# Holding the conditioning products of a hybrid decoder step behind two later norms

## The chip, the core and the metric

The kernel runs on one core of one Trainium2 chip. The metric is the device time of one execution in microseconds (us); smaller is better. The kernel before took 1204.66 us (median of three runs, 1202.11 to 1207.32). The engines are called PE (TensorE, the matrix products), DVE (VectorE), ACT (ScalarE), POOL (GpSimd) and SP (SyncE, which issues the DMA loads here).

## The reference

One step of a two-layer decoder for a prompt of 256 tokens and eight samples of four tokens each, 288 tokens in all, with a model width of 1024. Layer 0 mixes tokens by a gated delta rule (GDN), layer 1 by a state-space model (SSM). Each mixer is followed by a gated feed-forward part (FFN). Every part has a norm ahead of it, and each norm and each result is scaled and shifted by vectors made from a condition `c`:

```python
cs = jax.nn.silu(c)
for i in range(DEPTH):
    mod = cs @ p['w_mod'][i] + p['b_mod'][i]
    sh1, sc1, gt1, sh2, sc2, gt2 = [m[:, None, :] for m in jnp.split(mod, 6, axis=-1)]
    h = _rmsnorm(x, p['norm_mix'][i]) * (1 + sc1) + sh1
    ...
    x = x + gt1 * out
    h = _rmsnorm(x, p['norm_ffn'][i]) * (1 + sc2) + sh2
    x = x + gt2 * _swiglu(h, p['ffn_w_gate_up'][i], p['ffn_w_down'][i])
y = _rmsnorm(x, p['norm_final'])
```

Here `cs @ w_mod` gives twelve vectors (two layers, six each), the conditioning products. They hang on `c` alone and not on `x`, so that each may be computed at any time before its vector is used.

## The kernel before, in words

The activations stay on the chip, transposed: `x` has the 1024 channels as eight blocks (`k`) of 128 partitions by 288 tokens. The norm's output stands twice, `hh` and `hl`, a number rounded to the fast matmul format and what the rounding left over. Weights stream from memory.

**Weight chunks.** `chunk_load` (L267) takes 512 KB: four blocks of 128 rows by 256 columns. SP issues the load (L271) into a raw tile (`rw`, six tiles, shared with the conditioning loads). ACT writes the rounded copy `wh` (L87, four tiles), DVE the rest `wl` = `rw` - `wh` (L75, two tiles). `dense_chunk` (L285) then makes three products for each block and half: `wh` by `hh`, `wl` by `hh`, `wh` by `hl`; 24 in a chunk, into the accumulator `pd`. A chunk can be loaded and converted ahead with `load_early` (L282); `load32` (L361) does so for a 32-column piece.

**Stages.** In order: the first norm and the GDN mixer (to about 405 us, its output projection behind it), FFN0 (to 662), the SSM mixer (to 959), FFN1, and the final norm. The norms at the four seams are called norm 1 to norm 4 here: norm 3 stands between FFN0 and SSM, norm 4 between SSM and FFN1.

**A norm.** `Norm.add(k)` (L201) is called for every block of `x` as its projection ends: ACT squares the block, DVE adds it to `acc`. With the last block PE adds over the partitions by two products with ones into `ss` (the second is `self.mm`). Then `rstd` (L217) on ACT: logarithm, a load of the table of functions, exponential. `apply` (L223) goes on for each block: DVE makes `hu` (the scaled block), ACT `hh`, DVE `hl`. `hs` is the same for the sample tokens. The next stage's first product waits for the first `hh`. `apply` may issue an early chunk ahead of a given block (argument `at`).

**Conditioning products.** `mod_steps` (L147) is a generator for one vector: eight loads `wm` of 512 KB (L153), then after each second load a burst of eight calls on PE (`burst`, L64, at high priority), and as the last thing a tail: a copy `mt` on ACT, two transposes `pt` on PE, an addition on DVE. A vector has eight steps. `fill(n)` (L185) goes on by n steps, `ensure(r)` goes on to the end of the r-th vector. The vectors are made in the order in which they are used.

**What sets the order.** The code is written as generators which `weave` (L307) mixes in given shares; the SSM mixer's mix is a table of text lines, in which "m8" stands for eight steps of the conditioning products. The program order so made is given to a list scheduler, which sets each engine's final order by priority, with two means to bend it: `high_priority` and `issue_after`, which holds what is issued under it behind a given instruction. Tiles come from pools with a fixed number of buffers; a load waits until the tile's last reader is done.

Around norm 3, before, the calls were `ensure(8)`, `load32`, and an early chunk in `apply` at block 0. Around norm 4, before, there was one early chunk in `apply`, at block 4. The first steps of the next vectors came with `fill(4)` at the beginning of `ssm` and `fill(6)` at the beginning of FFN1.

Of the kernel before, what the change touches and what calls it, by code (L numbers as in the profile page):

```python
# [7 lines left out]
F32 = mybir.dt.float32  # L8
# [6 lines left out]
P = 128  # L15
NP_ = 256
# [4 lines left out]
KD = DM // P  # L21
# [6 lines left out]
def tile_hybrid_step(ctx: ExitStack, tc: tile.TileContext, I, O):  # L28
# [112 lines left out]
    def raw_tile(name):  # L141
        return wp.tile([P, 1024], F32, tag="raw", name=name, bufs=6)

    def sqt(name):
        return wp.tile([P, NT], F32, tag="sq", name=name, bufs=3)

    def mod_steps(l, s, m):  # L147

        pmod = pss.tile([P, 256], F32, tag="s", name=f"mod{l}{s}")
        rs_ = []  # L150
        for k in range(KD):
            r = raw_tile(f"wm{l}{s}{k}")
            SY.dma_start(r, I["w_mod"][l, k * P:(k + 1) * P, s * DM:(s + 1) * DM])  # L153
            rs_.append(r)
            if k % 2:

                burst([lambda q=q, k=k, r=r_: mm(pmod[32 * q:32 * q + 32, :], csT[:, k, :], r[:, 256 * q:256 * q + 256],
                                                 start=(k == 1), stop=(k == KD - 2))
                       for k, r_ in ((k, rs_[1]), (k - 1, rs_[0])) for q in range(4)])
                rs_.clear()  # L160
            if k < KD - 1:
                yield
        mt = sqt("mt")[:, 0:256]
        cp(mt, pmod)
        pt = pm([P, 2, P], "pt")
        for h in range(2):
            T.transpose(pt[:, h, :], mt[:, h * P:(h + 1) * P], ident)
        tt(m.rearrange("p (q h) r -> p h q r", h=2),
           pt.rearrange("p h (q r) -> p h q r", q=4)[:, :, :, 0:9],
           bmodT[:, l, s, :].rearrange("p (q h) -> p h q", h=2).unsqueeze(3).to_broadcast([P, 2, 4, 9]), ADD)  # L170
        if s in (1, 4):
            nw = nmix(l) if s == 1 else nffn(l)
            stt(m, m, 1.0, nw.unsqueeze(2).to_broadcast([P, KD, 9]), ADD, MUL)
        yield
# [10 lines left out]
    def fill(n=1):  # L185
        while n > 0 and todo:
            try:
                next(todo[0])
                n -= 1
                done[0] += 1  # L190
            except StopIteration:
                todo.pop(0)

    def ensure(rounds):
        fill(8 * rounds - done[0])
# [84 lines left out]
    early = {}  # L280

    def load_early(W, c0, k0, nk):  # L282
        early[c0, k0] = chunk_load(W, c0, k0, nk, 0)
# [23 lines left out]
    def weave(*work):  # L307

        work = [(w[0], w[1], w[2] if len(w) > 2 else 0) for w in work if w[0] is not None]
        top = max(n for _, n, _ in work)  # L310
        done = [0] * len(work)
        for i in range(1, top + 1):
            for w, (g, n, off) in enumerate(work):
                while done[w] * top < i * n:
                    done[w] += 1
                    if off:
                        with tc.high_priority(offset=off):
                            next(g, None)
                    else:
                        next(g, None)  # L320
        for g, _, off in work:
            for _ in g:
                pass
# [19 lines left out]
    def mods(n):  # L343
        for _ in range(n):
            fill(1)
            yield
# [181 lines left out]
    def gdn(gt1, nrm):  # L528
# [524 lines left out]
        ensure(6)  # L1053
        gst.close()

    def ffn(l, gt2, prev, nrm, late, n_late, n_mods):
        fst = ExitStack()
        fp = fst.enter_context(tc.tile_pool(name=f"ffn{l}", bufs=1))
        ah = fp.tile([P, KF, NT], F32R, name="ah")
        al = fp.tile([P, KF, NT], F32R, name="al")  # L1060
        W, WD = I["ffn_w_gate_up"][l], I["ffn_w_down"][l]
        def main():
            for p_ in range(KF // 2):
                pg, pu, gs = [], [], []
                yield from dense_g(pg, W, p_ * 256, KD, hh, hl)
                for m in range(2):
                    t = fp.tile([P, NT], F32, tag="gs", name="gs", bufs=4)
                    act(t, pg[m], AF.Silu)
                    gs.append(t)
                yield from dense_g(pu, W, FFN + p_ * 256, KD, hh, hl)  # L1070
                for m in range(2):
                    k = 2 * p_ + m
                    t = gs[m]
                    tt(t, t, pu[m], MUL)
                    cp(ah[:, k, :], t)
                    tt(al[:, k, :], t, ah[:, k, :].bitcast(F32), SUB)
            yield from out_proj(WD, ((0, KF),), KF, ah, al, gt2, nrm)

        work = late(fst)
        with prev.behind():  # L1080
            next(work)
        fill(n_mods[0])
        n_mods[1] = n_mods[1] if l == 0 else 96 - done[0]
        weave((main(), 136), (work, n_late), (mods(n_mods[1]), n_mods[1] + n_mods[2]) if n_mods[1] > 0 else (None, 0))
        fst.close()

    def late_tile(lp, name):
        return lp.tile([P, 1024], F32R, tag="st", name=name, bufs=4)

    def pattern(lp, src, outs, coefs, n, nm, vw=None):  # L1090
# [5 lines left out]
        for i, (o, (c_, m_)) in enumerate(zip(outs, coefs)):  # L1096
            u = (late_tile(lp, nm + "u")[:, 0:n] if i else t[:, n:2 * n]).bitcast(F32)
            act(u, src, AF.Copy, scale=m_)
            stt(o, vw(h_.bitcast(F32)), c_, vw(u), MUL, ADD)

    def late_gdn(fst):
        lp = fst.enter_context(tc.tile_pool(name="lateg", bufs=1))
        selB = lp.tile([P, 4, P], F32, name="selB")
        G.memset(selB, 0.0)
        for q in range(4):
# [42 lines left out]
    def ssm(gt1, nrm):  # L1148
# [320 lines left out]

        s0 = s0_products()  # L1470
        seq = chain_gens
        fill(4)
        weave((decays(), 6), (seq(*[bc_pair(p_) for p_ in range(4)]), 29), (mods(4), 18))
        smp_ = sample()
        proj = out_proj(I["ssm_w_out"][0], ((0, 12), (12, 16)), 16, yh, yl, gt1, nrm)
# [2 lines left out]
                     p=(lambda n: take(proj, n), 0),  # L1478
                     Z=(lambda n: mix(z_pair(n // 100, n // 10 % 10), 5, take(smp_, n % 10), n % 10), 9))
        for g, (line, more, side, smore, nc_, np_, tag) in enumerate((  # L1480
# [5 lines left out]
            main, n = plan(line, kinds)  # L1486
            side, m = plan(side, kinds)
            weave((core(g - 1, tag) if g else None, nc_), (main, n + more),
                  (prep(g) if g < 4 else None, np_), (side if m else None, m + smore))
        for _ in proj:  # L1490
            pass
        ensure(11)
        gst.close()

    def late_ssm(fst):
# [56 lines left out]
    nrm = Norm()  # L1552
# [92 lines left out]
    ffn(0, gt2, prev, nrm, late_gdn, 36, [6, 10, 9])  # L1645

    sh1, sc1, gt1, sh2, sc2, gt2 = mods1
    ensure(8)
    early[5120, 32] = load32(I["ssm_w_in"][0], 5120)
    nrm.apply(sc1, sh1, None, I["ssm_w_in"][0], 4096, (0,))  # L1650
    nrm = Norm()
    ssm(gt1, nrm)
    nrm.apply(sc2, sh2, None, I["ffn_w_gate_up"][1], 0, (4,))
    fin = ctx.enter_context(tc.tile_pool(name="fin", bufs=1))

    class Final:
# [35 lines left out]

    prev, nrm = nrm, Final()
    final[0] = nrm
    ffn(1, gt2, prev, nrm, late_ssm, 36, [6, 0, 9])
    nrm.finish()


# [28 lines left out]
```

## Time and profile before

| | |
|---|---|
| median of three runs | 1204.66 us (1202.11 to 1207.32) |
| the profiled execution | 1205.62 us |
| its span, first to last instruction | 1204.0 us |
| mean granted clock of PE | 0.979 of full |
| PE busy | 1138.1 us (95%) |
| DVE busy | 853.3 us (71%) |
| ACT busy | 629.8 us (52%) |

Times in the profile count from the start of the span. In a timeline a row gives the start, the time to the end, engine, line, operation, what is written from what, how many such instructions follow one another, and in brackets how long the engine had stood idle and what it had waited for. A row with a count shows a whole group. A burst of conditioning calls appears as 16 instructions, since each of the eight calls issues two.

### The profile page before, as it was taken

What the parts mean: (1) busy time and instruction counts of PE and PEld (TensorE: products, weight loads), DVE (VectorE), ACT (ScalarE), POOL (GpSimd) and SP (SyncE); (2) the same over time, 40 slices, a digit from 0 to 9 for tenths busy, and PEclk for the clock granted to TensorE, in tenths of its full rate; (3) what the DMA queues carried; (4) which work ended last, traced back from release to release, by engine and by line L of the source; (5) the groups of instructions that cost most, each with busy time, mean ns of one, the idle gap of its engine ahead of it and who ended that gap; (6) DMA issues with size and microseconds to landing.
All of it is one profiled execution on the core that took longest, in us unless ns stands there. A gap on an engine that the chain in (4) does not pass through costs nothing.

```text
span 1204.0 us, 23141 instructions
## 1 busy us (share of the span) xinstructions
PE 1138.1 (95%) x8634; PEld 1028.2 (85%) x8634; DVE 853.3 (71%) x2064; ACT 629.8 (52%) x1331; POOL 101.1 (8%) x273
## 2 busy tenths in 40 slices
PE   5899999999999999999999899999989989999996
PEld 3689778888978889999999788778869989999996
DVE  2878797888767785666664786678886787666654
ACT  3587445556544473434343675778734484444432
POOL 3121112122100100000000111001100010000000
PEclk8999999999999999999999899999989999999999
DMA  8765696633354689888655768667564579887771
GB/s 305 258 197 174 184 273 201 203 119 104 104 172 150 209 267 285 253 263 246 223 185 174 230 187 252 172 198 236 163 205 144 175 232 308 250 261 235 211 214 54
DMA packets 266724, 249.05 MB, mean 207 GB/s; under 512 B 12180, under 2 KB 252257, under 8 KB 266612
## 3 DMA queue, kind: packets, MB, share of 16 engines
q1 hardware_dynamic: 265980, 247.50, 66.4%
q8 instruction: 68, 1.11, 0.4%
q14 instruction: 44, 0.36, 0.1%
q10 hardware_dynamic: 632, 0.07, 0.0%
HBM read 226.64 MB, written 20.90 MB: 206 GB/s over the span
## 4 chain that ended last, share of the span: by engine, by line
PE 74%; DMA 9%; DVE 8%; ACT 6%; issue 2%; POOL 0%; SPq 0%; ACTq 0%; DVEq 0%; POOLq 0%
PE pd L62 56%; PE pch L62 4%; PE mod L62 3%; DMA wm<-in_w_mod_dram 3%; DMA D<-scumd 2%; DVE wl L75 1%; DVE cva L72 1%; ACT D L82 1%; DMA rw<-in_gdn_w_in_dram 1%; PE lu L62 1%; DMA rw<-in_ssm_w_in_dram 1%; ACT wh L87 1%; PE py L62 1%; DMA PP<-cumd 1%; DMA rw<-in_ffn_w_gate_up_dram 1%
## 5 line engine op out<-in xcount | busy, mean ns | idle before, releaser
L62 PE MATMUL pd<-hh,wh 128*128 128x288 f32 x1424 | 433.8, 306 | 10.6 <-ACT hh L87 9.1
L62 PE MATMUL pd<-hh,wl 128*128 128x288 f32 x1424 | 428.5, 301 | 2.5 <-DVE wl L75 2.5
L62 PE MATMUL pd<-hl,wh 128*128 128x288 f32 x1424 | 426.1, 301 | 1.7 <-DVE hl L72 1.5
L75 DVE TENSOR_TENSOR wl<-rw,wh 128x1024 fp32r<-128x1024 f32 (+2 forms) x258 | 309.9, 1201 | 163.6 <-PE pd L62 120.7
L87 ACT ACTIVATE wh<-rw 128x1024 fp32r<-128x1024 f32 (+2 forms) x258 | 267.9, 1040 | 270.2 <-PE pd L62 159.6
L62 PEld LDWEIGHTS pd<-hh,wh 128*128 128x128 f32 x1424 | 270.6, 190 | 27.9 <-issue 15.6
L62 PEld LDWEIGHTS pd<-hh,wl 128*128 128x128 f32 x1424 | 270.8, 190 | 6.0 <-DVE wl L75 3.8
L62 PEld LDWEIGHTS pd<-hl,wh 128*128 128x128 f32 x1424 | 270.6, 191 | 4.6 <-DVE hl L72 1.9
L62 PE MATMUL pd<-ah,wh 128*128 128x288 f32 x352 | 105.4, 299 | 0.0
L62 PE MATMUL pd<-al,wh 128*128 128x288 f32 x352 | 104.4, 297 | 0.0
L62 PE MATMUL pd<-ah,wl 128*128 128x288 f32 x352 | 104.4, 297 | 0.0
L72 DVE SCALAR_TENSOR_TENSOR cva<-ext,vT,cva 128x312 f32<-128x312 f32 x168 | 85.0, 537 | 8.9 <-ACT cva L82 8.3
L62 PEld LDWEIGHTS pd<-ah,wh 128*128 128x128 f32 x352 | 66.2, 188 | 1.2
L62 PEld LDWEIGHTS pd<-ah,wl 128*128 128x128 f32 x352 | 66.2, 188 | 0.0
L62 PEld LDWEIGHTS pd<-al,wh 128*128 128x128 f32 x352 | 66.2, 188 | 0.0
L62 PE MATMUL mod<-wm,csT 128*32 128x256 f32 x768 | 55.8, 415 | 8.1 <-DMA wm<-in_w_mod_dram 7.5
L62 PEld LDWEIGHTS mod<-wm,csT 128*32 128x32 f32 x768 | 21.5, 115 | 28.9 <-DMA wm<-in_w_mod_dram 11.0
L462 POOL COPY cvo<-ext 128x27 f32<-128x27 f32 x56 | 25.0, 446 | 220.0 <-ACT ext L87 219.4
L72 DVE SCALAR_TENSOR_TENSOR s0u<-s0u,elS,lu 128x128 f32<-128x128 f32 x128 | 36.3, 342 | 8.9 <-PE lu L62 8.5
L72 DVE SCALAR_TENSOR_TENSOR h0u<-h0u,elP,lsu 128x128 f32<-128x128 f32 x128 | 36.2, 342 | 7.4 <-PE lsu L62 6.5
L62 PE MATMUL pd<-ogh,wl 128*128 128x288 f32 x128 | 39.2, 307 | 2.2 <-DVE wl L75 2.2
L62 PE MATMUL pd<-ogh,wh 128*128 128x288 f32 x128 | 39.7, 311 | 0.0
(534 smaller groups left out, 1781.8 us busy)
## 6 DMA issues: line engine op xcount, KB each, us to landing
wm<-in_w_mod_dram SPq DMA_DIRECT2D x96, 512.0 KB
rw<-in_ffn_w_gate_up_dram SPq DMA_DIRECT2D x88, 512.0 KB
rw<-in_gdn_w_in_dram SPq DMA_DIRECT2D x48, 512.0 KB
rw<-in_ffn_w_down_dram SPq DMA_DIRECT2D x40, 512.0 KB
rw<-in_ssm_w_in_dram SPq DMA_DIRECT2D x40, 512.0 KB
s<-in_state_gdn_dram SPq DMA_DIRECT2D x16, 512.0 KB
rw<-in_gdn_w_out_dram SPq DMA_DIRECT2D x16, 512.0 KB
s0u<-in_state_gdn_dram SPq DMA_DIRECT2D x16, 512.0 KB
```

The lines of the kernel that those rows point to most:

```text
L62: return T.matmul(out, lhsT=lhsT, rhs=rhs, start=start, stop=stop)
L72: return V.scalar_tensor_tensor(out=out, in0=a, scalar=s, in1=b, op0=o0, op1=o1)
L75: V.tensor_tensor(out=out, in0=a, in1=b, op=op)
L82: return S.activation(out=out, in_=a, func=f, bias=bias, scale=scale)
L87: S.activation(out=out, in_=a, func=AF.Copy)
L462: G.tensor_copy(o[:, c % 4, :].rearrange("p (n s) -> p n s", s=3), e[:, 256:319].rearrange("p (n s) -> p n s", s=7)[:, :, 0:3])
```

## The change

The steps of a conditioning product are cut in another way: the first step now takes two loads and the first burst, bursts come in steps 1, 3, 5 and 7 (before: 2, 4, 6 and 8), and step 8 holds the tail alone. A new function `hold` makes seven steps of a product at a norm: the first three (four loads, two bursts) with spare tiles for their loads, then four under `issue_after` of the norm's last `ones` product, so that two bursts come behind it. At norm 3 the spare tiles are four of the pool that the work woven into FFN0 uses (`late_tile`); at norm 4 they are two `xf` and two `xt` tiles of the SSM mixer. The early loads move to the call of `hold`, and at norm 4 there are two early chunks (`k0` 0 and 4; before: one). The shares of steps in the SSM mixer and FFN1 are changed to fit.

```diff
+    spare = []
...
-            r = raw_tile(f"wm{l}{s}{k}")
+            r = spare.pop(0)() if spare else raw_tile(f"wm{l}{s}{k}")
...
-            if k < KD - 1:
+            if k:
                 yield
...
+    def hold(nrm, tiles):
+
+        spare.extend(tiles)
+        fill(3)
+        with tc.issue_after(nrm.mm.ins):
+            fill(4)
...
         weave((main(), 136), (work, n_late), (mods(n_mods[1]), n_mods[1] + n_mods[2]) if n_mods[1] > 0 else (None, 0))
+        if l == 0:
+            ensure(8)
+            early[5120, 32] = load32(I["ssm_w_in"][0], 5120)
+            load_early(I["ssm_w_in"][0], 4096, 0, 4)
+            hold(nrm, [lambda: late_tile(lps[0], "wms").bitcast(F32)] * 4)
         fst.close()
...
-        fill(4)
+        fill(1)
...
-                ("z01 z00 x00 x01", 3, "m8", 8, 0, 8, "m"),
+                ("z01 z00 x00 x01", 3, "m4", 8, 0, 8, "m"),
...
         ensure(11)
+        for k0 in (0, 4):
+            load_early(I["ffn_w_gate_up"][1], 0, k0, 4)
+        flat = lambda t: t.rearrange("p a b c -> p (a b c)")
+        hold(nrm, [lambda: f2(sp.tile([P, 4, NP_], F32, tag="xf", name="wmx"))] * 2 +
+             [lambda: flat(sp.tile([P, 2, 4, P], F32, tag="xt", name="wmt"))] * 2)
         gst.close()
...
-    ensure(8)
-    early[5120, 32] = load32(I["ssm_w_in"][0], 5120)
-    nrm.apply(sc1, sh1, None, I["ssm_w_in"][0], 4096, (0,))
+    nrm.apply(sc1, sh1)
...
-    nrm.apply(sc2, sh2, None, I["ffn_w_gate_up"][1], 0, (4,))
+    nrm.apply(sc2, sh2)
...
-    ffn(1, gt2, prev, nrm, late_ssm, 36, [6, 0, 9])
+    ffn(1, gt2, prev, nrm, late_ssm, 36, [0, 0, 9])
```

PE's order at norm 3, before, from the end of FFN0's last projection (`pd_7890`) to the first products of the SSM mixer:

```order
L62 MATMUL pd_7890<-al,wh 128x288
L62 MATMUL mod_8161<-wm_8164,csT 32x256 x4
L62 MATMUL mod_8161<-wm_8162,csT 32x256 x4
L62 MATMUL mod_8161<-wm_8176,csT 32x256 x4
L62 MATMUL mod_8161<-wm_8174,csT 32x256 x4
L62 MATMUL ss<-acc,ones 128x288
L62 MATMUL ss<-sq,ones 128x288
L443 MATMUL ph<-ident,hc 128x24 x4
L62 MATMUL pd<-hh,wh_8079 128x288
```

The same place now:

```order
L62 MATMUL pd_7890<-al,wh 128x288
L62 MATMUL mod_8089<-wms,csT 32x256 x16
L62 MATMUL ss<-acc,ones 128x288
L62 MATMUL ss<-sq,ones 128x288
L62 MATMUL mod_8089<-wm_8116,csT 32x256 x4
L62 MATMUL mod_8089<-wm_8114,csT 32x256 x4
L62 MATMUL mod_8089<-wm_8128,csT 32x256 x4
L62 MATMUL mod_8089<-wm_8126,csT 32x256 x4
L62 MATMUL pd<-hh,wh_8077 128x288
```

Sixteen calls stand ahead of the norm's sums in both; another sixteen stand behind them now, and the transposes `ph` of the convolution's history have left the place.

PE's order at norm 4, before, behind the SSM mixer's output projection:

```order
L62 MATMUL mod_11784<-wm_11787,csT 32x256 x4
L62 MATMUL mod_11784<-wm_11785,csT 32x256 x4
L62 MATMUL mod_11784<-wm_11799,csT 32x256 x4
L62 MATMUL mod_11784<-wm_11797,csT 32x256 x4
L62 MATMUL ss<-acc,ones 128x288
L62 MATMUL ss<-sq,ones 128x288
L1502 MATMUL lb<-ident,bB 128x128 x4
L62 MATMUL mod_11784<-wm_11811,csT 32x256 x4
L62 MATMUL mod_11784<-wm_11809,csT 32x256 x4
L62 MATMUL pd<-hh,wh 128x288
```

And now (`wmx` and `wmt` are the spare tiles):

```order
L62 MATMUL mod_11652<-wmx,csT 32x256 x8
L62 MATMUL mod_11652<-wmt,csT 32x256 x8
L62 MATMUL ss<-acc,ones 128x288
L62 MATMUL ss<-sq,ones 128x288
L62 MATMUL mod_11652<-wm_11679,csT 32x256 x4
L62 MATMUL mod_11652<-wm_11677,csT 32x256 x4
L62 MATMUL mod_11652<-wm_11691,csT 32x256 x4
L62 MATMUL mod_11652<-wm_11689,csT 32x256 x4
L1524 MATMUL lb<-ident,bB 128x128 x4
L62 MATMUL pd<-hh,wh 128x288
```

The fourth burst, which stood further on in FFN1, has come ahead of the first product as well.

DVE's order at norm 4 now, from the last but one block of `x` (its half `ru`) to the first `hu`:

```order
L75 TENSOR_TENSOR ru<-pd,modT_127 128x32
L75 TENSOR_TENSOR x<-x,ru 128x32
L75 TENSOR_TENSOR wl<-rw,wh 128x1024
L75 TENSOR_TENSOR acc<-acc,sq 128x288
L72 SCALAR_TENSOR_TENSOR x<-pd_11593,modT_127,x 128x256
L75 TENSOR_TENSOR acc<-acc,sq 128x288
L75 TENSOR_TENSOR ru<-pd_11593,modT_127 128x32
```

Before, the same rows stood there without `wl`; that conversion of the second chunk came between the `hu` and `hl` of blocks 2 to 4.

ACT's order at norm 4 now, from the last squares to the first `hh`:

```order
L82 ACTIVATE sq<-x 128x288 x2
L87 ACTIVATE wh<-rw 128x1024
L82 ACTIVATE sq<-x 128x288
L82 ACTIVATE rs<-ss,eps 128x288
L82 ACT_TABLE_LOAD
L82 ACTIVATE rs<-rs 128x288
L87 ACTIVATE wh<-rw 128x1024
L82 ACTIVATE hh<-hu,modT_128 128x256
```

Before, neither `wh` stood there: the row was `sq` three times, `rs`, the table load, `rs`, `hh`.

More of the change, by code (lines that the diff above doesn't have):

```diff
@@ L1099, in pattern @@
             stt(o, vw(h_.bitcast(F32)), c_, vw(u), MUL, ADD)
+    lps = []
     def late_gdn(fst):
         lp = fst.enter_context(tc.tile_pool(name="lateg", bufs=1))
+        lps.append(lp)
         selB = lp.tile([P, 4, P], F32, name="selB")
```

## Prediction

> **What bounds the kernel now.** I read the page first, then the engine shares, PE's waits, a table of stretches, and the timelines around the two norms that the change names.
>
> ```profile
> span 1204.0 us, 23141 instructions
> PE 1138.1 (95%) x8634; PEld 1028.2 (85%) x8634; DVE 853.3 (71%) x2064; ACT 629.8 (52%) x1331; POOL 101.1 (8%) x273
> ```
>
> PE is busy in 95% of the span, the next engine in 71%. No work is taken away here, so a gain can come only from PE's idle time or from its clock. PE's waits, in all, in number and the longest:
>
> ```profile
> PE pd L62 <- ACT hh L87: 9.1, 4, 3.9
> PE mod L62 <- DMA wm<-in_w_mod_dram: 7.5, 6, 3.1
> ```
>
> The four entries to a projection (one behind each norm, waiting for `hh`) are the largest sum. The stretches show what they cost in clock; the columns are busy time and instructions of PE, PEld, DVE, ACT and POOL, then granted clock, DMA share and GB/s:
>
> ```profile
> 405.00:425.00 20.00, 18.03 (x151) 14.66 (x151) 15.52 (x41) 10.19 (x18) 3.84 (x7) 1.00 0.77 245
> 662.00:666.00 4.00, 4.00 (x46) 2.42 (x44) 3.54 (x10) 1.06 (x3) 0.98 (x2) 1.00 0.31 33
> 666.00:670.00 4.00, 0.15 (x3) 0.04 (x1) 1.74 (x5) 3.08 (x7) 0.87 (x5) 0.92 0.86 305
> 670.00:676.30 6.30, 6.23 (x26) 6.26 (x27) 5.82 (x15) 3.92 (x8) 0.00 (x0) 0.51 0.82 300
> 890.00:903.00 13.00, 10.56 (x70) 6.32 (x70) 8.32 (x26) 2.93 (x9) 0.00 (x0) 0.61 0.64 205
> 963.00:966.40 3.40, 0.79 (x13) 0.30 (x6) 1.91 (x6) 2.50 (x5) 0.00 (x0) 0.99 1.03 344
> 966.40:969.80 3.40, 2.96 (x12) 2.61 (x11) 2.21 (x7) 1.53 (x3) 0.00 (x0) 0.50 1.09 361
> ```
>
> After FFN0 (norm 3) PE works 0.15 of 4 us and then goes at 0.51 of its clock for 6.3 us. After the SSM mixer (norm 4) it works 0.79 of 3.4 us and then goes at 0.50. After the GDN mixer (the first row), whose gap holds conditioning bursts already, the clock stays at 1.00. There the first projection waits only 0.81:
>
> ```profile
> 419.82 0.40 PE L62 MATMUL pd<-hh,wh 128*128 128x288 f32 x1 [0.81 <-ACT hh L87]
> ```
>
> **Norm 3, part by part.** PE before:
>
> ```profile
> 662.69 1.93 PE L62 MATMUL mod<-wm,csT 128*32 128x256 f32 x32
> 665.14 0.65 PE L62 MATMUL ss<-sq,ones 128*128 128x288 f32 x2
> 665.72 0.42 PE L443 MATMUL ph<-ident,hc 24*128 24x24 f32 x4
> 670.07 0.58 PE L62 MATMUL pd<-hh,wh 128*128 128x288 f32 x1 [3.92 <-ACT hh L87]
> 670.69 0.44 PE L62 MATMUL pd<-hh,wh 128*128 128x288 f32 x1
> 670.93 0.44 PE L62 MATMUL pd<-hh,wl 128*128 128x288 f32 x1
> ...
> 676.36 0.29 PE L62 MATMUL pd<-hh,wl 128*128 128x288 f32 x1
> 676.49 0.30 PE L62 MATMUL pd<-hl,wh 128*128 128x288 f32 x1
> ...
> 679.36 1.07 PE L62 MATMUL mod<-wm,csT 128*32 128x256 f32 x16
> 684.10 1.07 PE L62 MATMUL mod<-wm,csT 128*32 128x256 f32 x16
> ```
>
> Sixteen calls (two bursts, 1.93 us) stand ahead of `ss` in both kernels. The other two bursts of that product came at 679.36 and 684.10, amid projections; now they stand behind `ss`, ahead of the first `pd`. This has three consequences.
>
> First, 2 x 1.0 us of PE work moves into time in which PE stood still: 2.0. Second, the idle 3.92 shrinks by 1.93, to 2.0, or about 2.3 as the `ph` transposes (665.72) move away too. Third, the clock: from 670.07 to 676.21 26 products start 0.24 us apart (670.69 to 670.93); at full clock they start 0.13 apart (676.36 to 676.49). That is 26 x 0.106 = 2.8, of which some 0.3 can't be had, since the last `hl` holds the products back:
>
> ```profile
> 666.23 0.24 ACT L87 ACTIVATE hist<-ph 128x96 f32<-128x96 f32 x1
> 675.51 0.48 DVE L72 SCALAR_TENSOR_TENSOR hl<-hu,modT,hh 128x256 fp32r<-128x256 f32 x1 [0.18 <-ACT hh L82]
> ```
>
> The `hist` copy leaves the chain ahead of the table load: 0.2. Upper bound 2.0 + 2.5 + 0.2 = 4.7.
>
> Does the clock hold over an idle of 2.2? The nearest rows say that it may not:
>
> ```profile
> 345.33 0.61 PE L62 MATMUL pd<-ogh,wl 128*128 128x288 f32 x1 [2.18 <-DVE wl L75]
> 345.73 0.44 PE L62 MATMUL pd<-ogl,wh 128*128 128x288 f32 x1
> 345.97 0.44 PE L62 MATMUL pd<-ogh,wh 128*128 128x288 f32 x1
> ```
>
> After 2.18 us of idle the products go 0.24 apart. Half-clock stretches come as 3.4 us or two of these (966.4 to 969.8; 670 to 676.3 less its edge). I take one stretch: 3.4 / 0.24 = 14 products, 14 x 0.106 = 1.5 lost of the 4.7.
>
> What comes late instead: the four spare loads free raw tiles for the next product's loads, so that on SP three of these (two before) stand ahead of weight chunk 2 and chunk 3 waits for a tile that the next product's first burst frees, about 677 by my estimate from the count of calls between; `hc`, and so `hist`, comes behind it. ACT before:
>
> ```profile
> 682.82 0.65 ACT L82 ACTIVATE cva<-ext,vT 128x312 f32<-128x312 f32 x1
> 684.02 1.06 ACT L87 ACTIVATE wh<-rw 128x1024 fp32r<-128x1024 f32 x1 [0.55 <-DMA rw<-in_ssm_w_in_dram]
> ```
>
> `hist` is a PE transpose at about 683.7 now, so the first convolution starts near 684.2, 1.4 later; weights were the wait at 684.02 already and PE now arrives 2 to 4 us sooner. Its price lies between 0 (PE has other projections meanwhile) and 2.7, which leaves 0.5 of the remaining 3.2, what the better filled gap is worth before the first convolution is asked for. I take 1.0, between the 0.55 at 684.02 and the 1.4. **Norm 3: 4.7 - 1.5 - 1.0 = 2.2, bounds 0.5 to 4.7.**
>
> The Trainium skill ("TensorE: Matmul & The Clock Gate", Part 1: The HAM clock gate) says that the array drops to half clock after an idle window of about 3.4 us. By that rule 2.2 us would cost no clock, and the sum would be 1.5 better; the 2.18 at 345.33 and the 2.62 below speak against it as a threshold.
>
> **Norm 4.** PE before:
>
> ```profile
> 958.97 1.93 PE L62 MATMUL mod<-wm,csT 128*32 128x256 f32 x32
> 962.53 1.07 PE L62 MATMUL mod<-wm,csT 128*32 128x256 f32 x16
> 966.22 0.50 PE L62 MATMUL pd<-hh,wh 128*128 128x288 f32 x1 [2.62 <-ACT hh L87]
> 969.97 0.40 PE L62 MATMUL pd<-hh,wh 128*128 128x288 f32 x1 [0.61 <-ACT hh L82]
> 971.22 0.40 PE L62 MATMUL pd<-hl,wh 128*128 128x288 f32 x1 [0.47 <-DVE hl L72]
> 974.34 0.40 PE L62 MATMUL pd<-hh,wl 128*128 128x288 f32 x1 [0.34 <-DVE wl L75]
> ```
>
> DVE, ACT and SP before:
>
> ```profile
> 959.08 0.48 DVE L72 SCALAR_TENSOR_TENSOR x<-pd,modT,x 128x256 f32<-128x256 f32 x1
> 969.55 1.22 DVE L75 TENSOR_TENSOR wl<-rw,wh 128x1024 fp32r<-128x1024 f32 x1 [1.19 <-ACT wh L87]
> ```
>
> ```profile
> 968.46 1.06 ACT L87 ACTIVATE wh<-rw 128x1024 fp32r<-128x1024 f32 x1 [1.87 <-DMA rw<-in_ffn_w_gate_up_dram]
> ```
>
> ```profile
> 960.10 11.07 SPq L271 DMA_DIRECT2D rw<-in_ffn_w_gate_up_dram  x6
> ```
>
> Here three of four bursts stood at the gap already, so only one more enters it: 1.0. The second early chunk spares what waited for it: 0.61 + 0.47 + 0.34 = 1.4, and the `wl` at 969.55 leaves the row of `hu` and `hl`. If PE's stop ahead of `ss` and the one behind it keep each below 2 us, the half-clock stretch goes too: 12 products x 0.106 = 1.3. Together 3.7.
>
> Against it: that `wl` now stands on DVE ahead of the last `x`, and waits for the output projection's last products (959.0) to free its buffer. So the last `x`, the last square, `ss`, `rs` and all behind them, PE's first `pd` too, come 1.2 + 0.2 = 1.4 later. On ACT a `wh` of a third chunk stands between the second `rs` and the first `hh`; `hh` waits 0.9 for `hu` anyway, so that 1.06 costs 0.2 if its weights are there. Another 0 to 2 is open, by its landing. **Gain 3.7 - 1.4 - 0.2 = 2.1 at best, 0.1 with the open 2; I take 1.2.**
>
> **Elsewhere.** Every conditioning product now issues its second load a step earlier, and its bursts come a step earlier, all through boot, GDN and both FFNs. The number of calls and loads stays. It could help or harm the worst such wait:
>
> ```profile
> 890.33 1.08 PE L62 MATMUL mod<-wm,csT 128*32 128x256 f32 x16 [3.06 <-DMA wm<-in_w_mod_dram]
> ```
>
> The 890 to 903 row above (0.61) holds what follows it. In that stage the product load that PE waits for keeps its place behind three others on SP, though one of these is now for a spare tile. If that wait fell wholly, 3.06 plus some 10 us of half clock would be up to 4 us of gain; if each later product waited as long anew, as much of loss. I take -0.5 (a loss), for SP carries one load more ahead of others in several places, bounds -4 to +4.
>
> **Sum.** 2.2 + 1.2 - 0.5 = 2.9 us less. The profiled execution took 1205.62 (span 1204.0), so 1202.7; the runs' median is 1204.66, 0.96 below it, so 1201.8. A measurement here tells 0.5% (6.0 us) from no change: 1198.6 and 1210.7 are the bounds.
>
> **Rivals.**
>
> *Full clock at norm 3.* The gap at 412 to 420 keeps 1.00; if 2.2 us of idle do too and the late weights are hidden, norm 3 gives 4.7, norm 4 1.2 to 2.1: 1204.66 - 4.7 - 1.2 = 1198.8, with 2.1 there 1197.9. For it: the filled gap at norm 2. Against it: 345.33. This is the outcome that the Trainium skill's rule above leads to.
>
> *The entry of SSM takes it back.* PE, 2 to 4 us ahead at 680, waits for chunk 3's `wh` and the convolution: for it the 0.55 at 684.02; against it the many projections PE can do first. Norm 3 0.5, norm 4 0.5, elsewhere -0.5: 1204.2.
>
> *Slower: the third `wh` at norm 4.* The first `hh` is queued on ACT behind a conversion that waits for a load. Before, the load issued at 960.10 let `wh` start at 968.46. Landing so again, first `hh` comes at about 969.6 and first `pd` at 970.5, 4.3 later than now, less the 1.4 of stalls spared: +2.9. The stop of over 4 us brings two half-clock stretches for one: +1.4. Norm 3 taken back as above: 1204.66 + 4.3 - 0.5 = 1208.5, and up to 1212 if the product loads elsewhere are late too. It decides once the load lands after about 966. For it: DMA runs at 1.03 to 1.09 there. Against it: only `nfb` stands ahead of it on SP, no product load as before.
>
> *That the change doesn't do what it says:* the order shows the bursts behind `ss` at both places; 0.02.
>
> **Chances.** Forecast 0.45; full clock 0.21; taken back 0.18; slower mechanism 0.14; no effect 0.02. Half of the full-clock case and a tenth of the forecast (an 890 stretch healed) pass 1198.6, and I allow 0.05 for an unseen gain: 0.20 faster. Half of the slower case passes 1210.7, with 0.05 for loads that come late in boot or GDN: 0.12 slower. The rest, 0.68, is no change. The range 1195.5 to 1208.5 holds the forecast, nearly all of the full clock and half of the slow case.
>
> **What would show it.** Norm 3: 32 calls in two groups around `ss`, first `pd` within 0.3 of 670, and the clock after it at 1.00 or one 3.4 us stretch of 0.5; first `cva` 1 to 2 us later against `pd`'s start. Norm 4: last `x` about 1.4 later, a `wh` ahead of the first `hh`; the stalls 0.61, 0.47 and 0.34 gone. Wrong if the first `pd` at norm 4 comes over 3 us later against the end of the output projection, if half-clock time there grows, or if boot, GDN or the 890 stage moves by more than 4 us.

## The result and the profile after

The changed kernel took 1196.25 us (median of six runs, 1194.03 to 1199.06) against 1206.32 us of the kernel before (median of six, the three of 1204.66 among them). The ratio is 0.9919, 95% interval 0.9900 to 0.9938. Two later sets, each beside its own runs of the kernel before, gave 0.9923 (0.9895 to 0.9950) and 0.9943 (0.9921 to 0.9964). Four single executions that took 1257 to 2733 us (of the kernel before, norm 4 alone, the xf tiles alone and the changed kernel) are left out of the ratios of this document. So the change makes the kernel faster by 0.6% to 0.8%, 7 to 10 us. The forecast was 1201.8 us, with a range down to 1195.5: the time lies in the range, but near its lower end, and the forecast's sum of 2.9 us holds less than half of the gain. The question is where the other 4 to 7 us came from.

The page of the profile after, and PE's largest waits in it (sum, number, longest):

```profile
span 1192.3 us, 23162 instructions
PE 1132.9 (95%) x8634; PEld 1023.1 (86%) x8634; DVE 849.9 (71%) x2064; ACT 629.3 (53%) x1331; POOL 104.2 (9%) x273
...
PE pd L62 <- ACT hh L87: 7.6, 4, 2.9
PE mod L62 <- DMA wm<-in_w_mod_dram: 3.8, 5, 2.4
```

**Norm 3.** PE's timeline of the changed kernel, and the table of stretches around it (columns as in the prediction; the clock is the third number from the end):

```profile
658.15 1.93 PE L62 MATMUL mod<-wms,csT 128*32 128x256 f32 x32
661.18 1.93 PE L62 MATMUL mod<-wm,csT 128*32 128x256 f32 x32
665.39 0.37 PE L62 MATMUL pd<-hh,wh 128*128 128x288 f32 x1 [2.28 <-ACT hh L87]
...
661.00:665.40 4.40, 2.12 (x35) 0.97 (x33) 1.83 (x6) 3.19 (x6) 0.57 (x3) 1.00 0.93 325
665.40:668.80 3.40, 3.40 (x26) 3.40 (x27) 3.40 (x10) 1.59 (x4) 0.00 (x0) 1.00 0.96 316
```

The gap is 2.28 us in place of 3.92, and in this execution the clock behind it stays at 1.00.

**Norm 4.** PE's sums before, then PE now:

```profile
960.83 0.75 PE L62 MATMUL ss<-acc,ones 128*128 128x288 f32 x2
```

```profile
949.05 1.07 PE L62 MATMUL mod<-wmx,csT 128*32 128x256 f32 x16
952.31 0.72 PE L62 MATMUL ss<-acc,ones 128*128 128x288 f32 x2 [1.32 <-DVE acc L75]
953.63 1.93 PE L62 MATMUL mod<-wm,csT 128*32 128x256 f32 x32
957.75 0.40 PE L62 MATMUL pd<-hh,wh 128*128 128x288 f32 x1 [1.60 <-ACT hh L87]
963.22 0.40 PE L62 MATMUL pd<-hh,wh 128*128 128x288 f32 x1 [0.75 <-ACT hh L82]
```

The two conversions on ACT now:

```profile
950.56 1.06 ACT L87 ACTIVATE wh<-rw 128x1024 fp32r<-128x1024 f32 x1 [1.32 <-DMA rw<-in_ffn_w_gate_up_dram]
955.90 1.04 ACT L87 ACTIVATE wh<-rw 128x1024 fp32r<-128x1024 f32 x1
```

From the bursts ahead of the sums to `ss` it takes 3.26 us (before: 958.97 to 960.83, 1.86), so the norm starts 1.40 later. The `wh` at 950.56 is that of the third chunk (its load was issued at 947.09), the one at 955.90, ahead of the first `hh`, that of the fourth; the fourth doesn't wait for its load, the third does (1.32). Of the three stops inside the first projection (0.61, 0.47, 0.34) one of 0.75 is left, and the clock stays at 1.00 from 957.75 to 971.40.

**A place that the change's lines don't touch.** Near the end of the SSM mixer PE does the last group's products, two bursts and the last `z` projection, and then waits for `yh`, the normed output that the output projection reads. In the kernel before, PE (from the second burst to the first product with `yh`) and ACT there:

```profile
882.40 1.07 PE L62 MATMUL mod<-wm,csT 128*32 128x256 f32 x16
903.38 0.40 PE L62 MATMUL pd<-yh,wh 128*128 128x288 f32 x1 [0.42 <-ACT yh L87]
...
889.04 1.06 ACT L87 ACTIVATE wh<-rw 128x1024 fp32r<-128x1024 f32 x1 [1.26 <-DMA rw<-in_ssm_w_out_dram]
890.01 0.61 ACT L82 ACTIVATE sqs<-y1s 128x512 f32<-128x512 f32 x1
901.64 0.69 ACT L82 ACTIVATE D<-D,scum 128x128 f32<-128x128 f32 x2 [1.03 <-DMA D<-scumd]
902.70 0.63 ACT L87 ACTIVATE yh<-y1s 128x512 fp32r<-128x512 f32 x1
```

And in the changed kernel:

```profile
873.18 1.07 PE L62 MATMUL mod<-wm,csT 128*32 128x256 f32 x16
892.62 0.40 PE L62 MATMUL pd<-yh,wh 128*128 128x288 f32 x1
...
880.67 0.63 ACT L82 ACTIVATE sqs<-y1s 128x512 f32<-128x512 f32 x1 [0.66 <-DVE y1s L75]
881.86 1.06 ACT L87 ACTIVATE wh<-rw 128x1024 fp32r<-128x1024 f32 x1 [0.25 <-DMA rw<-in_ssm_w_out_dram]
891.38 0.63 ACT L87 ACTIVATE yh<-y1s 128x512 fp32r<-128x512 f32 x1 [1.68 <-DVE y1s L75]
```

It takes 20.98 us before and 19.44 us now. Before, two ACT instructions that wait for loads (`wh`, and `D`, the decay of the last group) stood ahead of two that the sample tokens' part of `yh` hangs on (`sqs` and `yh`); now they stand behind them. The scheduler's order on ACT, before:

```
L87 ACTIVATE wh<-rw 128x1024
L82 ACTIVATE sqs<-y1s 128x512
L87 ACTIVATE yh<-xf 128x256 x2
L82 ACTIVATE sqa<-xf 128x256
L82 ACTIVATE D<-D,scum 128x128 x2
L82 ACTIVATE D<-D,c_8153 128x128
L87 ACTIVATE yh<-y1s 128x4x4x32
```

and of the changed kernel:

```
L82 ACTIVATE sqs<-y1s 128x512
L87 ACTIVATE yh<-xf 128x256
L87 ACTIVATE wh<-rw 128x1024
L87 ACTIVATE yh<-xf 128x256
L82 ACTIVATE sqa<-xf 128x256
L87 ACTIVATE yh<-y1s 128x4x4x32
L82 ACTIVATE ssq<-xf 128x256
```

`yh` at 902.70 ran at once when the `D` group ahead of it, which had waited 1.03 for its load, was through. The Trainium skill ("TensorE: Matmul & The Clock Gate", Part 1, the paragraph on engine queue depths) says that ACT's queue is strictly first in, first out; the rows agree.

### The profile page after: what moved, and what is told of

The parts are those of the page before. It is cut to its first block, busy times and chain, and to the rows that moved or that the text cites. A ratio compares the mean times of both kernels' runs of the same rounds, so it can differ in the third digit from the quotient of the medians.

```text
span 1192.3 us, 23162 instructions
## 1 busy us (share of the span) xinstructions
PE 1132.9 (95%) x8634; PEld 1023.1 (86%) x8634; DVE 849.9 (71%) x2064; ACT 629.3 (53%) x1331; POOL 104.2 (9%) x273
## 5 line engine op out<-in xcount | busy, mean ns | idle before, releaser
L62 PEld LDWEIGHTS pd<-hh,wh 128*128 128x128 f32 x1424 | 268.4, 189 | 23.8 <-issue 12.2
L62 PE MATMUL mod<-wm,csT 128*32 128x256 f32 x704 | 51.5, 419 | 4.2 <-DMA wm<-in_w_mod_dram 3.8
L62 PEld LDWEIGHTS mod<-wm,csT 128*32 128x32 f32 x704 | 20.2, 117 | 22.2 <-issue 8.4
L87 ACT ACTIVATE ext<-pd 128x256 f32<-128x256 f32 x112 | 27.6, 292 | 21.5 <-PE pd L62 18.4
```

Source lines behind the costliest of these rows:

```text
L62: return T.matmul(out, lhsT=lhsT, rhs=rhs, start=start, stop=stop)
L87: S.activation(out=out, in_=a, func=AF.Copy)
```

## The experiments

The theory after the two traces: (1) the re-cut steps gave the GDN part the 4.5 us by which the changed kernel's first profile is ahead at norm 3; (2) norm 3 and (3) norm 4 give what the profile shows. The rivals stand in the expectations. After the first four kernels below, ACT's order in the tail took the place of (1).

The times of each stage, from one profile each, are set together here. Their marks are the starts of the bursts ahead of the sums at norm 3 and norm 4, and the end of the span; the tail runs from the second burst near 880 to the first `yh` product. The last column is the ratio to the kernel before, with its interval. The three rows of the change are one program: they differ by 7.5 us at norm 3, by 5.0 between the norms, by 1.8 in the tail and by 0.2 behind norm 4, so that smaller differences of two rows in a column say nothing.

| kernel | to norm 3 | norm 3 to norm 4 | norm 4 to end | tail | ratio |
|---|---|---|---|---|---|
| before | 662.7 | 296.3 | 245.0 | 21.0 | |
| steps alone | 661.2 | 299.2 | 245.2 | 21.3 | 1.0004 (0.9987 to 1.0021) |
| filler at norm 3 | 661.9 | 297.5 | 244.5 | 22.8 | 1.0008 (0.9989 to 1.0026) |
| norm 3 alone | 661.8 | 296.5 | 245.8 | 22.5 | 0.9979 (0.9963 to 0.9996) |
| norm 4 alone | 660.0 | 293.5 | 243.4 | 17.8 | 0.9962 (0.9948 to 0.9976) |
| old steps elsewhere | 661.9 | 294.6 | 243.2 | 22.0 | 0.9971 (0.9957 to 0.9985) |
| change | 658.2 | 290.9 | 243.3 | 19.4 | 0.9919 (0.9900 to 0.9938) |
| change, second | 662.0 | 295.9 | 243.5 | 19.4 | 0.9923 (0.9895 to 0.9950) |
| change, third | 665.7 | 291.9 | 243.4 | 17.6 | 0.9943 (0.9921 to 0.9964) |
| xf tiles alone | 661.6 | 298.0 | 243.9 | 23.8 | 0.9996 (0.9980 to 1.0012) |
| xt tiles alone | 661.7 | 290.1 | 243.8 | 17.6 | 0.9953 (0.9936 to 0.9971) |
| xf alone, D behind yh | 660.1 | 295.8 | 243.5 | 20.0 | 0.9957 (0.9938 to 0.9976) |
| wl behind x | 660.3 | 293.3 | 242.6 | 18.7 | 0.9909 (0.9881 to 0.9937) |
| wl behind x, second | 659.8 | 289.0 | 242.6 | 17.6 | 0.9922 (0.9905 to 0.9940) |

### The steps alone

```diff
-            if k < KD - 1:
+            if k:
                 yield
```

> The kernel before with one edit: a product's first step takes two loads and the first burst, the tail stands alone in the eighth step. No product is held at a norm. Theory A (the 4.5 us that the changed kernel was ahead at the start of norm 3 come from this edit, which moves the product loads and bursts in the GDN part): 3 to 5 us less than before, the 2.18 us wait for wl near 345 gone, the 3.92 us gap at norm 3 still there. Theory B (those 4.5 us are the spread between executions, or come from tile placement): within 1.5 us of before. Theory C (the forecast): 0.5 us more.

Measured: 1206.77 us, ratio 1.0004. Theory A falls, theory B stands: the 4.5 us at norm 3 are no property of the change. The wait of 2.18 us at 345.33 is gone, as theory A asked, and the whole is no shorter for it (at most 1.6 us). The three profiles of the changed kernel reach norm 3 at 658.2, 662.0 and 665.7, the others at 659.8 to 662.7.

### Norm 3 alone

```diff
-        for k0 in (0, 4):
-            load_early(I["ffn_w_gate_up"][1], 0, k0, 4)
...
-        hold(nrm, [lambda: f2(sp.tile([P, 4, NP_], F32, tag="xf", name="wmx"))] * 2 +
-             [lambda: flat(sp.tile([P, 2, 4, P], F32, tag="xt", name="wmt"))] * 2)
...
-    nrm.apply(sc2, sh2)
+    nrm.apply(sc2, sh2, None, I["ffn_w_gate_up"][1], 0, (4,))
...
-    ffn(1, gt2, prev, nrm, late_ssm, 36, [0, 0, 9])
+    ffn(1, gt2, prev, nrm, late_ssm, 36, [6, 0, 9])
```

> The changed kernel without the held product and the two early chunks at norm 4 (one early chunk in apply at block 4, and six steps at the start of FFN1, as before). Theory A: the GDN part 4.5 us and norm 3 about 5.3 us less, so 9 to 10 us less than before, and 1 to 2 us more than the changed kernel. Theory B: 5 to 6 us less than before. The forecast's sizes (2.2 at norm 3, 0.5 lost elsewhere): 1.7 us less.

Measured: 0.9979, 2.5 us less than before (0.5 to 4.5). With (1) gone, this is what norm 3 gives: the forecast's 2.2 stands, the 5.3 that theory A took from the first profile lies outside the interval. The tail is the old one, 22.5.

### Norm 4 alone

```diff
-        if l == 0:
-            ensure(8)
-            early[5120, 32] = load32(I["ssm_w_in"][0], 5120)
-            load_early(I["ssm_w_in"][0], 4096, 0, 4)
-            hold(nrm, [lambda: late_tile(lps[0], "wms").bitcast(F32)] * 4)
...
-        fill(1)
+        fill(4)
...
-                ("z01 z00 x00 x01", 3, "m4", 8, 0, 8, "m"),
+                ("z01 z00 x00 x01", 3, "m8", 8, 0, 8, "m"),
...
-    nrm.apply(sc1, sh1)
+    ensure(8)
+    early[5120, 32] = load32(I["ssm_w_in"][0], 5120)
+    nrm.apply(sc1, sh1, None, I["ssm_w_in"][0], 4096, (0,))
```

> The changed kernel without the held product at norm 3 (the calls there as before). Theory A: the GDN part 4.5 us and norm 4 about 1.8 us less, so 6 us less than before; the 3.92 us gap at norm 3 and its half clock are back. Theory B: 1 to 2 us less than before. The forecast: 0.7 us less.

Measured: 0.9962, 4.6 us less (2.9 to 6.3). By its one profile only 1.6 of it lie behind norm 4 (243.4 against 245.0). The rest stands ahead of norm 4, where this kernel has the short tail of 17.8 us. That was the first sign that the size came from there.

### The old steps for the ten other products

```diff
-            if k:
+            if (k if (l, s) in ((1, 2), (1, 5)) else k < KD - 1):
                 yield
```

> The changed kernel, with the new step cut for the two held products alone; the ten others are cut as before. Theory A: the gain of the GDN part is lost, so 6 to 7 us less than before and some 4 us more than the changed kernel. Theory B: no difference from the changed kernel beyond 1.5 us. The 2.18 us wait near 345 is back under A.

Measured: 0.9971, 3.5 us less than before (1.8 to 5.2). Both norms are as in the change, and yet it lies 3 to 6 us above it. The loss is the one that theory A expected, though the kernel is not the 6 to 7 us below the one before that theory A gave it, and the reason is another: this kernel reaches norm 3 at 661.9, like the rest. The wait near 345 is back (2.71 at 346.24), but taking that wait away was worth at most 1.6 us in the kernel with the steps alone. It has the long tail (22.0) and, on ACT, the old order: `D` ahead of `yh`.

### The change again

The kernel of the change, twice more, beside other kernels.

> The changed kernel once more, beside its own runs of the kernel before, to measure its size with more executions. Theory A (the parts add: norm 3 alone gave 2.5 us, norm 4 alone 4.6, the new step cut alone 0): 7 us less than before. Theory B (the parts help each other): 9 to 10 us less, as in its first six executions.

> The changed kernel beside the two before it and the one after it, on the same chip: 7 to 9 us less than before; a further profile for the times of each stage.

Measured: 1198.98 and 1199.91 us, ratios 0.9923 and 0.9943. Theory A and B can't be told apart by these. The second profile shows how much one execution differs from another with the same instructions in the same order: behind norm 3 one half-clock stretch, where the first had none.

```profile
665.01 1.93 PE L62 MATMUL mod<-wm,csT 128*32 128x256 f32 x32
669.22 0.37 PE L62 MATMUL pd<-hh,wh 128*128 128x288 f32 x1 [2.27 <-ACT hh L87]
...
669.20:672.60 3.40, 3.38 (x16) 3.40 (x17) 3.40 (x10) 1.61 (x4) 0.00 (x0) 0.60 1.00 329
```

### A filler in the gap at norm 3

The kernel before with sixteen products that nobody reads, behind the sums:

```diff
+    dum = pm([P, 256], "dum")
+    with tc.issue_after(nrm.mm.ins), tc.high_priority(offset=4000):
+        for i in range(4):
+            for q in range(4):
+                mm(dum[32 * q:32 * q + 32, :], csT[:, i, :], x[:, i, 0:256], start=(i == 0), stop=(i == 3))
     nrm.apply(sc1, sh1, None, I["ssm_w_in"][0], 4096, (0,))
```

> The kernel before with 16 extra products of the same form (their result is used by nothing) behind norm 3's sums, ahead of the first projection: the gap is filled as in the change, but no work is moved into it, no load is moved and nothing else of the change is there. Theory A (the clock alone is worth half of what norm 3 gives): half-clock time at 666 to 676 falls from 3.4 to 0 or 1.7 us of lost work, the first pxt comes 1.5 to 3 us earlier behind norm 3, the whole 1 to 3 us less. Rival (the moved work is all of it): no change within 1 us. Rival (the gap of 2.3 us that is left still brings two half-clock windows): no change, and the clock after norm 3 stays 0.5.

PE's timeline and the stretch behind the gap in this kernel, then two stretches behind the unfilled gap in the kernel with the steps alone, and two behind the same unfilled gap (3.92 us) in the kernel with norm 4 alone:

```profile
664.92 1.93 PE L62 MATMUL dum<-x,csT 128*32 128x256 f32 x32
669.13 0.37 PE L62 MATMUL pd<-hh,wh 128*128 128x288 f32 x1 [1.92 <-ACT hist L87]
...
669.10:672.50 3.40, 3.37 (x17) 3.40 (x18) 3.40 (x10) 1.63 (x5) 1.21 (x3) 0.63 1.05 408
```

```profile
668.50:671.90 3.40, 2.59 (x20) 1.20 (x20) 3.40 (x10) 1.67 (x4) 0.00 (x0) 0.58 1.04 394
671.90:675.30 3.40, 3.40 (x17) 3.20 (x14) 2.00 (x6) 2.25 (x4) 0.00 (x0) 0.50 1.09 356
```

```profile
667.40:670.80 3.40, 3.39 (x22) 1.86 (x23) 3.40 (x10) 1.60 (x4) 0.00 (x0) 0.54 1.03 387
670.80:674.20 3.40, 3.40 (x28) 3.40 (x28) 2.33 (x6) 2.26 (x4) 0.00 (x0) 1.00 1.09 354
```

Measured: ratio 1.0008 (0.9989 to 1.0026), at best 1.3 us less than before. The filled gap has one half-clock stretch. The unfilled one has two in the kernel before and with the steps alone, but one with norm 4 alone, so a single profile doesn't show that the filler took one away. The first `pxt` comes 79.4 us behind the bursts ahead of the sums (80.8 before), just short of what theory A asked. A gain of more than 1.3 us from filling the gap without moving work lies outside the interval. That the rest of what norm 3 gives is the moved work is argued and not shown: the 2.5 us of norm 3 alone may be as little as 0.5.

### The wl behind the last x

The changed kernel with the second early chunk's `wl` held on DVE behind the last addition to `x` (`residual` and `tt` are made to hand on their instruction, `lastx`; `load_early` hands `nrm` on for `k0` 4):

```diff
             cp(wh[:, :n], r[:, :n])
-            tt(wl[:, :n], r[:, :n], wh[:, :n].bitcast(F32), SUB)
+            with tc.issue_after(lastx[0].ins) if nrm else ExitStack():
+                tt(wl[:, :n], r[:, :n], wh[:, :n].bitcast(F32), SUB)
```

> The changed kernel, with one conversion moved: the wl of the second early chunk at norm 4 is held behind the last addition to x on DVE. By the prediction's step that this wl makes the norm 4 chain 1.2 to 1.4 us late (and the wh ahead of hh 0.2 more): PE's wait for acc ahead of ss (1.32) goes, the first pd of FFN1 comes 1.2 to 1.6 us earlier against the end of the output projection, 1 to 1.5 us less than the changed kernel. Rival (DVE's chain of hu and hl, not its start, sets the first projections' end): the first pd comes earlier, the stop before a later pd grows by as much, no change in the whole.

> The kernel with the wl of the second early chunk behind the last x, beside the changed kernel once more. If FFN1's part is 0.7 us shorter, as in its first profile, the whole is 0.5 to 1 us below the changed kernel; the rival (the first 2 us between their medians were the spread) has them within 0.5 us.

PE and ACT at norm 4 in the second profile of it:

```profile
948.84 1.07 PE L62 MATMUL mod<-wmx,csT 128*32 128x256 f32 x16
952.08 0.75 PE L62 MATMUL ss<-sq,ones 128*128 128x288 f32 x2 [0.62 <-ACT sq L82]
956.88 0.40 PE L62 MATMUL pd<-hh,wh 128*128 128x288 f32 x1 [1.60 <-ACT hh L87]
...
950.63 1.06 ACT L87 ACTIVATE wh<-rw 128x1024 fp32r<-128x1024 f32 x1 [1.59 <-DMA rw<-in_ffn_w_gate_up_dram]
951.60 0.42 ACT L82 ACTIVATE sq<-x 128x288 f32<-128x288 f32 x1
```

Measured: 1197.03 and 1196.68 us, 2.0 and 3.2 below the changed kernel measured beside it. That is more than the 0.5 to 1 us asked for in the second set, but the intervals of the ratios overlap, so that the size is not settled. PE's wait for `acc` is gone, and the first `pd` comes 8.04 us behind the bursts in place of 8.70: 0.66 sooner, not 1.2 to 1.6. The stop before a later `pd` doesn't grow (0.75 in the change, 0.75 and 0.76 here), so the rival of the first set falls. The stretch from norm 4 to the end is 0.7 to 0.9 us shorter in both profiles. The edit also let the fourth chunk's `wh` fall behind the first `hh`; the first `hh` starts 0.51 behind its `hu` with it and without it, so this is worth nothing. The prediction's step is confirmed in kind and halved in size: the `wh` of the third chunk stands on ACT ahead of the last square, waits 1.59 for its load, and holds the last sum for 0.62. In both sets this kernel has the lowest time.

### Which spare tiles

The changed kernel with only the two `xf`, and then with only the two `xt`, as spare tiles at norm 4:

```diff
-        hold(nrm, [lambda: f2(sp.tile([P, 4, NP_], F32, tag="xf", name="wmx"))] * 2 +
-             [lambda: flat(sp.tile([P, 2, 4, P], F32, tag="xt", name="wmt"))] * 2)
+        hold(nrm, [lambda: f2(sp.tile([P, 4, NP_], F32, tag="xf", name="wmx"))] * 2)
```

> The changed kernel with two spare tiles at norm 4 (the two xf; the loads that went to the two xt take raw tiles). The bursts held at norm 4 stay where they are. What moves is the order of PE at the end of SSM's last group: the sum over the group (apn with dg) stands behind all but four of the py products, as in the kernel before and in the kernel with norm 3 alone; in the changed kernel seven stand behind it. Theory A (this order, which the xt tile's load brought about, is the 3 us that the SSM stage gained beside the two gaps): from the second burst of the product in that tail to the first yh product 21 to 23 us in place of 18 to 19.5, 2.5 to 3.5 us more than the changed kernel, FFN1's part unchanged within 0.5. Theory B (the held bursts alone, or the loads off the raw tiles, make the gain): no more than 1 us over the changed kernel.

> The counterpart: two spare tiles at norm 4, the two xt, while the loads that went to the two xf take raw tiles. PE's order at the end of SSM's last group is that of the changed kernel. Theory A: 18 to 19.5 us from the second burst to the first yh product, and the whole within 1 us of the changed kernel. Theory B: the same loss as with the xf tiles alone, since both take two loads back to raw tiles.

With the `xf` tiles alone, PE and ACT in the tail:

```profile
878.99 1.07 PE L62 MATMUL mod<-wm,csT 128*32 128x256 f32 x16
888.74 1.86 PE L62 MATMUL apn<-ones,sqs 128*128 128x1 f32 x8 [2.03 <-ACT sqs L82]
902.80 0.40 PE L62 MATMUL pd<-yh,wh 128*128 128x288 f32 x1 [1.99 <-ACT yh L87]
...
887.11 1.06 ACT L87 ACTIVATE wh<-rw 128x1024 fp32r<-128x1024 f32 x1 [1.68 <-DMA rw<-in_ssm_w_out_dram]
901.83 0.40 ACT L82 ACTIVATE D<-D,scum 128x128 f32<-128x128 f32 x1 [3.10 <-DMA D<-scumd]
902.14 0.61 ACT L87 ACTIVATE yh<-y1s 128x512 fp32r<-128x512 f32 x1
```

With the `xt` tiles alone, PE:

```profile
878.03 1.07 PE L62 MATMUL mod<-wm,csT 128*32 128x256 f32 x16
895.61 0.40 PE L62 MATMUL pd<-yh,wh 128*128 128x288 f32 x1
```

Measured: 0.9996 with `xf` alone, 0.9953 with `xt` alone. With `xf` alone the tail takes 23.8 us, PE stands 2.03 for `sqs` and 1.99 for `yh`, and the whole gain of the change is gone, although sixteen calls are held at both norms and the stretch behind norm 4 is nearly as short as in the change (243.9). It lies 6.2 us above the changed kernel beside it, twice what theory A gave it. With `xt` alone the tail takes 17.6 and the whole is 0.7 us above the changed kernel, as theory A has it. Both take two loads back to raw tiles, so theory B falls. The expectation named PE's order as the cause. But in this stage the two kernels differ in order on PE (by a few rows), on ACT, on DVE and in the loads that SP issues; this pair does not tell which of them counts.

### D behind yh

The kernel with the `xf` tiles alone, and on ACT the last `D` of the last group held behind the sample part of `yh` (its load is issued where it was):

```diff
+                if (g, pp) == (3, 3):
+                    held.append(steps())
...
+            if g == 3:
+                with tc.issue_after(ylast[0].ins):
+                    for _ in held[0]:
+                        pass
```

Here `steps` are the ACT instructions on that `D` and `ylast` is the instruction that writes `yh`.

> The kernel with the xf spare tiles alone (as slow as the kernel before), with one edit: on ACT the last group's last D work is held behind the sample part of yh, which stood behind one D that waited 3.10 us for its load. Nothing else on any engine changes its order. Theory A (ACT's order there, loads ahead of what PE waits for, is what the SSM stage gains in the changed kernel): PE's wait of 1.99 for yh ahead of the first yh product goes, from the second burst to that product 21 to 22 us in place of 23.8, 2 to 3 us less than with the D ahead; the rest of the 6 us to the changed kernel stays, since the wh ahead of sqs still waits for its load (2.03 of PE's idle time). Rival (the D is needed as soon by the last py): PE waits as much longer for py further on, no change within 1 us.

PE and ACT with `D` behind:

```profile
879.87 1.07 PE L62 MATMUL mod<-wm,csT 128*32 128x256 f32 x16
889.74 1.87 PE L62 MATMUL apn<-ones,sqs 128*128 128x1 f32 x8 [1.91 <-ACT sqs L82]
899.84 0.40 PE L62 MATMUL pd<-yh,wh 128*128 128x288 f32 x1 [0.64 <-ACT yh L87]
...
899.16 0.63 ACT L87 ACTIVATE yh<-y1s 128x512 fp32r<-128x512 f32 x1 [1.05 <-DVE y1s L75]
901.33 0.69 ACT L82 ACTIVATE D<-D,scum 128x128 f32<-128x128 f32 x2 [1.54 <-DMA D<-scumd]
```

The fourth burst and a stretch behind `yh` with `D` ahead (the `xf` tiles alone), then a stretch behind `yh` with `D` behind:

```profile
893.00 1.93 PE L62 MATMUL mod<-wm,csT 128*32 128x256 f32 x16 [0.91 <-DMA wm<-in_w_mod_dram]
...
904.30:907.70 3.40, 3.40 (x16) 3.40 (x16) 1.38 (x2) 2.01 (x6) 0.00 (x0) 0.52 0.26 77
```

```profile
903.20:906.60 3.40, 3.40 (x26) 3.18 (x24) 2.28 (x3) 3.11 (x8) 0.00 (x0) 1.00 0.26 80
```

Measured: 0.9957 (0.9938 to 0.9976), against 0.9996 (0.9980 to 1.0012) with `D` ahead, each beside its own runs of the kernel before. In the two traces PE, DVE, POOL and SP keep their order; only ACT's differs. One instruction group's place on ACT is worth 0.4%, 4.7 us, which the two intervals together leave between 1.7 and 7.7. Theory A stands; its 2 to 3 us lie within that. The traces show the larger part of it. PE's wait for `yh` is 1.35 shorter (1.99 to 0.64), and the half-clock stretch behind the stop (0.52 from 904.30) is gone, by the prediction's price of such a stretch another 1.5: together 2.9, an estimate. The tail falls by more, from 23.8 to 20.0 us, but the rest of that stands ahead of the moved instructions and is not the edit's: the fourth burst waited 0.91 for its load in one profile and not in the other, and the `py` products ahead of `yh` ran at a lower clock (0.61 from the fourth burst to `yh`, against 0.88). PE still waits 1.91 for `sqs`, behind the `wh`; what that place of `wh` is worth was not measured by itself.

## Why the prediction was right or wrong

- **What bounds the kernel:** right. PE's count of products is as before (8634). In the first profile its idle time is 6.5 us shorter (65.9 to 59.4) and its busy time 5.2 (1138.1 to 1132.9).
- **Norm 3, 2.2 taken, bounds 0.5 to 4.7:** right; 2.5 us (0.5 to 4.5) measured with norm 3 alone. The gap is 2.28, as worked out (about 2.3). The one half-clock stretch that was charged appears in one of the three profiles of the change. The first `cva` comes 14.9 us behind the first `pd` (680.30 on ACT), 12.8 before: 2.1 later, a little over the 1 to 2 forecast. In the first 32 us behind the bursts PE stops for 0.69 us (for `ext`) and 0.53 (for `cvo`), before for 0.31, so the 1.0 taken for it was about right.
- **Norm 4, 1.2 taken, best 2.1:** right; 1.5 to 1.7 from the bursts to the end (243.3 to 243.5 against 245.0; the other kernels with the old norm 4 have 244.5 to 245.8). The last sums come 1.40 later, as forecast. The `wl` ahead of the last `x` was the right cause of only half of that: the `wh` ahead of the last square, which the prediction gave no price, is the other half. The 0.2 for the `wh` ahead of the first `hh` measures 0.
- **Elsewhere, -0.5 taken, bounds -4 to +4:** here the prediction failed. The step looked at this very stage (the row at 890.33) but only for the wait of the bursts, and took a small loss, because the load for them keeps its place on SP. The stage gave 3.9 us instead: inside the bounds, with the other sign, and by a step that the sum does not have. The bursts' wait hardly fell: the third burst waits 1.88 to 2.35 in the three profiles of the change (3.06 before), and the fourth, which did not wait before, 0.25 to 1.74. What moved was the order there, ACT's above all: `sqs` and `yh` came ahead of two instructions that wait for loads. The loads into the two `xt` tiles and the re-cut steps brought this about together, for without either (the `xf` tiles alone; the old steps elsewhere) the old order stays, and the steps alone have it too.
- **What the tail gave.** It takes 21.0 to 23.8 us in the six kernels of the old order (mean 22.2) and 17.6 to 19.4 in the seven profiles of the new one (mean 18.3): 3.9 less (2.7 against the one profile of the kernel before), and 3.7 if it is counted to the end of the output projection, since two `py` products come behind the first `yh` product in the new order. With 2.5 for norm 3 and 1.6 for norm 4 that makes 8.0, against 6.9 to 9.8 measured. That the place of `D` and `yh` on ACT costs time is shown by the kernel that moves them alone. How much of the 3.9 it is in the change is not shown: that kernel took away a wait of PE of 1.99 us for `yh`, and in the kernel before PE waits there for 0.42 in its one profile. The place of `sqs` and the rows that moved with it on DVE, PE and SP were not tried alone. The kernel with the `xf` tiles alone has both norms and gains only 0.5 us (2.4 less to 1.4 more) where the norms should give 4.1; its tail, 1.6 above the mean of the old order, takes part of that, and the rest is open.
- **The rivals.** The time came out near where "full clock at norm 3" had it (1197.9 to 1198.8). The clock behind norm 3 did stay at 1.00 in two of the three profiles of the change, but norm 3 alone gave 2.5 (0.5 to 4.5) and not 4.7, and the tail is in none of that rival's terms: the number agrees in part by luck. "Taken back" and "slower" did not come. The third chunk's `wh`, which "slower" had ahead of the first `hh`, stands ahead of the last square instead and waits 1.32 for its load; the `wh` ahead of the first `hh` is the fourth chunk's and started at 955.90 without a wait, and the first `pd` came at 957.75.
- **The clock rule.** Behind the idle of 2.28 or 2.27 us at norm 3 half clock came in the second profile of the change, with no other difference in order, and not in the first. Over the ten profiles with this gap it came in four. By the Trainium skill ("TensorE: Matmul & The Clock Gate", Part 1: The HAM clock gate), where half clock comes after an idle window of about 3.4 us, such a gap should cost no clock. As a threshold of idle time 3.4 us is too high for these rows. The Trainium skill also says there that the window runs freely, so that the number of slow products varies from run to run; that agrees. A single profile can't price the clock of such a gap.

## What to carry to other kernels

When a scheduler sets the order, compare the order of every engine in every stage that has idle time, not only around the lines of the diff: spare buffers for two loads at norm 4, with a new cut of small steps, changed the order on ACT some 70 us ahead of that norm, and that stage gave about as much (3.9 us by the traces) as the two gaps that the change aimed at (2.5 and 1.6). On an engine that works strictly in order, look at each wait for a load and ask what stands behind it; here moving one such group of instructions gave 0.4%. Do not read a difference between two single profiles stage by stage: the same program reached norm 3 at 658, 662 and 666 us.

## What the runs showed that was not expected

- A half-clock stretch of 3.4 us behind an idle of 2.3 us comes in some executions and not in others of one program (clock 1.00 at 665.40 in the first profile, 0.60 at 669.20 in the second; four of ten profiles with this gap have it). Behind the unfilled gap of 3.92 us one or two such stretches came. Filling it without moving work into it gave no measurable time.
- The gain of the parts does not add by name: the step cut gives nothing alone (1.0004), and yet without it in the other products the change loses more than half of its gain (0.9971). What the traces show beside it is the order on ACT, which goes back to the old one; the norms stay as in the change.
